# One layer of a convolution and pooling mixer: the gate rows' scaling moves to the w_out stage, the weight sums to VectorE, and two starts are reordered

## The chip, the cores and the metric

The kernel runs on one core of a Trainium2 chip. The metric is the device time of one execution in microseconds (us). The kernel before takes 1025.55 us, the median of three runs that lie between 1024.84 and 1026.43. A separate execution was recorded by the hardware profiler, and all instruction times below come from that one.

TensorE multiplies matrices into PSUM banks, VectorE and ScalarE do elementwise work (ScalarE also the activation functions), GpSimd does elementwise work and issues DMAs, and SyncE only issues DMAs. Each engine takes its instructions in the order of its own queue.

## The reference

```python
def layer(h, p, conv_hist, pool_hist, pos, ...):
    hn = rmsnorm(h, g_mix)
    proj = hn @ w_in                                    # 1024 -> 3072
    hA, bA, cA, zA, vB, zB = jnp.split(proj, 6 parts of 512)
    yA, new_conv = short_conv_mixer(hA, bA, cA, zA, conv_hist, conv_w, conv_b)
    yB, new_pool = pooling_mixer(vB, zB, pool_hist, pos, pool_w, pool_scale)
    h = h + jnp.concatenate([yA, yB], axis=-1) @ w_out  # 1024 -> 1024
    gate = jax.nn.sigmoid(rmsnorm(h, g_ple) @ w_ple_gate)
    return h + (p @ w_ple) * gate, new_conv, new_pool   # then a final rmsnorm
```

The convolution mixer is a causal width-3 convolution of `c * h`, times `b * silu(z)`. The pooling mixer takes trailing means over windows of 2, 4, 8 and 16 frames minus the frame itself, multiplies each group of 128 channels by its own 128 x 128 matrix, scales it, and multiplies by `silu(z)`. There are 2048 frames of a new stream and 32 frames of a running one, 1024 wide, all in 32-bit floats. The gate's norm weight `g_ple` belongs to the rows of `w_ple_gate`: scaling a row of the gate's weights by `g_ple` is the same as scaling the normalised frames.

## The kernel before

**Products.** Each 32-bit operand is split into a rounded high part and a low remainder: `split` (L75) casts on ScalarE (L77) and subtracts on VectorE (L78). A product is then three TensorE passes (high by high, high by low, low by high). On top of that, most products are done in the manner of Strassen and Winograd: a two-by-two block product takes seven products instead of eight, with sums and differences of the blocks formed beforehand, called S1 to S4 on one side and T1 to T4 on the other. `seven` (L197) does this for a pair of frame tiles in the w_out and gate stages: it calls `product` (L154: 12 matmuls of 512 columns), `carry` (which takes a PSUM bank out to be added later) and `out` (which adds it).

**The projection.** The frames are cut into five blocks of 416 columns, in three groups: blocks 0 and 1, blocks 2 and 3, block 4. Every group is worked through in four units, one for each 128 channels. The first unit of the first group and all four units of the last group are `plain`: full products for zb, v, c, h, za and b in this order, each with 24 matmuls of 416 columns to a block (L527). After the v product the pooling is done on VectorE (L695, L707), its result `pl` is split into `pp` (L77, L78) in a long and, in the last group, a short second piece, and `pm` (L673 to L675) multiplies `pp` by the group's matrix; in the last group `pm` stands between the h and the za products. The other units use `pair` (L802) three times, for zb with v, c with h, za with b; its carry is ScalarE's copy (L814) and its out VectorE's add (L817). Their weights come from `pair_weights` (L481): the sum `s_t` (L503) and the difference (L490) of two weight tiles run on GpSimd in the first group and on VectorE in the second. In the first group the two results are also stored to memory (`kept`, L508 and L509), and the second group loads those that were kept. Beside these units, generators work off other jobs step by step: `second_block` (L560) normalises the second block's frames and transposes them on TensorE (`turn`, L371) into the operands `B0` during the first unit; `next_columns` and `last_block` (`aside`) prepare the frames of the later groups and write them to memory with `to_memory` (L434).

**The gate's rows and other early work.** In the last group, each unit is followed in the program by `early_sums` (L943: T1 to T4 of w_out's weights, on VectorE at L164) and by two calls of `scale_gate` (L933): 128 rows of the gate's weights, 512 KB, are loaded on SyncE's queue (L939), multiplied by `g_ple` on ScalarE (L940) and stored to `g_d` from ScalarE's queue (L941). `embedding` (L100) prepares `p @ w_ple` for frame tiles: transposes (L125), cast of `pps`, 12 matmuls (L143), copy to `eout` (L145), store (L146). Four tiles (EARLY) are done before the w_out stage, 13 after it.

**The w_out stage** (from L1065). Sixteen frame tiles go in eight pairs through `seven`, then a single short tile. `prep_h` forms a pair's S operands by `frame_parts` (L167), one pair ahead. The carry adds the frames x to the PSUM bank (`c_o`, L1086). For the first pair, the top half of w_out is in SBUF already, T1 to T4 come from `early_sums`, and the bottom half (`wo_q`, L280) is loaded at its start; the 22 and 21 quarters are laid out after the first product (`rest`). After the stage come the late embedding tiles, the gate's weights read back from `g_d`, and eight pairs of the gate product with the final norm.

A scheduler orders the instructions of each engine at build time, so the order in a queue can differ from the order of the program.

Of the kernel before, what the change touches and what calls it, by code (L numbers as in the profile page):

```python
# [15 lines left out]
P = 128  # L16
D = 1024
# [12 lines left out]
EARLY = 4  # L30
# [4 lines left out]
def trunk(ctx, tc, x_p, x_s, c_conv, c_pool, p_p, p_s, g_mix, w_in, conv_w, conv_b, pool_w,  # L35
# [131 lines left out]
    def frame_parts(cmb, tmp, name, a11, a12, a21, a22):  # L167
# [19 lines left out]
        put("S1", s1)  # L187
# [9 lines left out]
    def seven(name, A, W, carry, out, between={}, late=False):  # L197
# [6 lines left out]
        X, Y, Z = (bank(f"{c}_{name}") for c in "xyz")  # L204
        product(X, A["11"], W["11"], P, True)
# [13 lines left out]
        product(Z, A["S1"], W["T1"], P, True)  # L219
        c3 = carry(Z, (1, 1))  # L220
# [67 lines left out]
    with ExitStack() as s1:  # L288
# [37 lines left out]
        gm_row = ring4(raws, "gm_row")[:1]  # L326
# [107 lines left out]
        def to_memory(mem, name, src, at, n):  # L434
            t = xin.tile([P, KH, 2, P], F32R, tag="t", name=name)
            put(t[:, :, :, :n], src)
            nc.gpsimd.dma_start(mem[:, :, :, at:at + n], t[:, :, :, :n].bitcast(F32))
# [43 lines left out]
        def pair_weights(gi, ka, kb, j, name, ring, s_ring):  # L481
# [8 lines left out]
            sub = lambda e, o, x, y: e.tensor_tensor(o, x, y, op=ALU.subtract)  # L490
# [8 lines left out]
            else:  # L499
                rb = raw_weight(kb, j, f"{name}b", ring)  # L500
                a21, a22 = rb[:, :KH], rb[:, KH:]
                eng = nc.gpsimd if gi == 0 else nc.vector
                eng.tensor_tensor(s_t, a21, a22, op=ALU.add)  # L503
                sub(eng, a21, a11, a21)
# [7 lines left out]
            def make(q):  # L512
                if q == "S2":
                    sub(nc.vector, a11, s_t, a11)
                if q == "S4":
                    sub(nc.vector, a12, a12, a11)
                t = wtile(f"w_{name}_{q}")
                put(t, src[q])
                return t
# [40 lines left out]
        def second_block():  # L560

            spans = [(c, slice(c * P, min(NB, c * P + P))) for c in range(4)]
            xs = []
            for c, cs in spans:
                x, lo, n = short0, DEC, DEC
                if c < 3:
                    x, lo, n = x_tile(f"1_{c}", [x_rows(1, c)]), 0, P
                    normal(x)
                xs.append((x, slice(lo, lo + n)))
                for half, q in enumerate(("12", "22")):  # L570
                    put(B0[q][:, :, :, cs], turn(x, half, f"pt1_{c}_{half}")[:, :, xs[c][1]])
                yield
# [50 lines left out]
        class Unit:  # L623
# [98 lines left out]
            def plain(self):  # L722
# [21 lines left out]
                if len(tbs) > 1:  # L744

                    wc = weights("c", j, f"c{tag}")
                    for b in blocks:
                        zb_block(b)
                        v_block(b)
                        if b:  # L750
                            self.mix(b - 1)
                            next(second)
                        c_block(b)
                        if b == 0:
                            for _ in range(4):
                                next(second)
# [176 lines left out]
        def scale_gate(k):  # L933

            t = ring4(raws, f"gs_{k}")
            nc.sync.dma_start(t, w_gate.rearrange("(q k c) n -> k q c n", q=4, k=KC)[k])  # L939
            nc.scalar.activation(t, t, AF.Copy, scale=vec[:, 100 + k:101 + k])  # L940
            nc.scalar.dma_start(g_d[k * P:k * P + P], t)  # L941

# [21 lines left out]
        def early_embedding():  # L964
# [3 lines left out]
            def ring(what, i):  # L968
                if what == "pps":
                    return pps_tile(i)  # L970
                if what == "out" and i == EARLY - 1:
# [13 lines left out]
        def next_columns(*cs):  # L985

            load_ahead(1, cs[0])
            for c, after in zip(cs, cs[1:] + (None,)):
                dst = lambda q, src, n: to_memory(p_d[q], f"{q}_1_{c}", src, c * P, n)
# [32 lines left out]
        for gi, tbs in enumerate(GROUPS):  # L1022
# [17 lines left out]
            for j in range(4):  # L1040
# [25 lines left out]
    with ExitStack() as s2:  # L1066
        pool = lambda name, bufs: s2.enter_context(tc.tile_pool(name=name, bufs=bufs, reuse_waits="tile"))
        w3, st, xh, qa, ss, cmb = (pool(*a) for a in (
            ("w3", 1), ("st", 4), ("xh", 3), ("qa", 2), ("ss", 3), ("cmb", 8)))
# [260 lines left out]
```

## Time and profile before

| | |
|---|---|
| median of three runs | 1025.55 us |
| the profiled execution, its own time | 1027.12 us |
| its span | 1025.3 us |
| TensorE matmuls busy | 950.1 us, 93% |
| VectorE busy | 718.8 us, 70% |
| ScalarE busy | 477.7 us, 47% |
| GpSimd busy | 152.0 us, 15% |
| mean granted TensorE clock | 0.972 |
| mean DMA rate | 185 GB/s |

The span is what the profile covers; the device time is 1.8 us more. In the rows that the prediction shows, a row of the timeline gives the start, the time that the group of instructions spans, the engine (SPq and ACTq are the DMA issues of a queue), the line, the operation, the tile written and the tiles read, the shapes, and how many instructions are in it; in brackets stands how long the engine was idle just before and what ended that. A row of the table of waits says who waited for whom, how long in all, how often, and the longest one. The granted clock is the share of full speed that TensorE had.

### The profile page before, as it was taken

What the parts mean: (1) busy time and instruction counts of PE and PEld (TensorE: products, weight loads), DVE (VectorE), ACT (ScalarE), POOL (GpSimd) and SP (SyncE); (2) the same over time, 40 slices, a digit from 0 to 9 for tenths busy, and PEclk for the clock granted to TensorE, in tenths of its full rate; (3) what the DMA queues carried; (4) which work ended last, traced back from release to release, by engine and by line L of the source; (5) the groups of instructions that cost most, each with busy time, mean ns of one, the idle gap of its engine ahead of it and who ended that gap; (6) DMA issues with size and microseconds to landing.
All of it is one profiled execution on the core that took longest, in us unless ns stands there. A gap on an engine that the chain in (4) does not pass through costs nothing. (4 is left out here: it accounts for less than half of the span.)

```text
span 1025.3 us, 13116 instructions
## 1 busy us (share of the span) xinstructions
PE 950.1 (93%) x4631; PEld 848.0 (83%) x4631; DVE 718.8 (70%) x1181; ACT 477.7 (47%) x874; POOL 152.0 (15%) x260
## 2 busy tenths in 40 slices
PE   7899998988999999997787897999999989999995
PEld 6899898978999999997787885788887768888883
DVE  6598798969576777675445464965653686888874
ACT  6454454534444544443343345433332685555553
POOL 2214433530100110000000000100000000211212
PEclk9999999999999999999799899999999999999998
DMA  9236586593954556345755738546246574665651
GB/s 258 53 125 186 158 269 192 176 283 119 421 194 133 163 163 199 119 176 162 217 157 161 209 122 325 165 158 211 89 158 197 191 284 137 215 233 184 206 196 51
DMA packets 127951, 190.03 MB, mean 185 GB/s; under 512 B 8268, under 2 KB 97612, under 8 KB 126605
## 3 DMA queue, kind: packets, MB, share of 16 engines
q1 hardware_dynamic: 115805, 137.34, 42.5%
q0 software_dynamic: 10352, 45.56, 13.0%
q10 hardware_dynamic: 1728, 6.29, 1.7%
q8 instruction: 36, 0.59, 0.2%
q14 instruction: 30, 0.25, 0.1%
HBM read 129.06 MB, written 60.10 MB: 184 GB/s over the span
## 5 line engine op out<-in xcount | busy, mean ns | idle before, releaser
L527 PE MATMUL x_ch<-B,w_ch_S 128*128 128x416 f32 x168 | 37.1, 374 | 6.5 <-ACT c_s L814 6.5
L77 ACT CAST y_S<-y_fS 128x512 fp32r<-128x512 f32 x32 | 19.6, 622 | 46.2 <-PE x_o L154 27.6
L143 PE MATMUL e<-wq,pps 128*128 128x512 f32 (+1 forms) x156 | 40.0, 408 | 0.5 <-ACT pps L77 0.5
L527 PEld LDWEIGHTS x_ch<-B,w_ch_S 128*128 128x128 f32 x168 | 33.7, 202 | 7.7 <-ACT c_s L814 7.2
L527 PE MATMUL x_zbv<-B,w_zbv_S 128*128 128x416 f32 x168 | 35.3, 360 | 3.0 <-ACT zs L814 3.0
L154 PE MATMUL x_o<-wo_b,y_S 128*128 128x512 f32 x128 | 35.9, 393 | 1.1 <-DVE c_o L1086 1.1
L364 DVE SCALAR_TENSOR_TENSOR xt<-xt,rstd_x,g_bc 128x1024 f32<-128x1024 f32 (+2 forms) x18 | 23.1, 1282 | 18.0 <-POOL rstd_x L73 16.7
L154 PE MATMUL x_g<-wg_b,g_S 128*128 128x512 f32 x128 | 35.5, 389 | 0.0
L527 PEld LDWEIGHTS x_zbv<-B,w_zbv_S 128*128 128x128 f32 x168 | 31.9, 192 | 4.1 <-ACT zs L814 3.7
L527 PE MATMUL z_zbv<-B,w_zbv_S 128*128 128x416 f32 x168 | 34.8, 357 | 0.0
L69 POOL TENSOR_SCALAR ms_f<-ssq_f 128x1 f32<-128x1 f32 x16 | 9.1, 571 | 173.1 <-ACT junk L88 173.1
L143 PEld LDWEIGHTS e<-wq,pps 128*128 128x128 f32 (+1 forms) x156 | 28.3, 189 | 7.4 <-ACT pps L77 0.8
L527 PE MATMUL z_ch<-B,w_ch_S 128*128 128x416 f32 x168 | 34.4, 354 | 0.0
L527 PE MATMUL x_zab<-B,w_zab_S 128*128 128x416 f32 x168 | 34.1, 351 | 0.0
L527 PE MATMUL z_zab<-B,w_zab_S 128*128 128x416 f32 x168 | 34.0, 351 | 0.0
L673 PE MATMUL pm<-pp,pw 128*128 128x416 f32 x20 | 7.8, 399 | 27.2 <-ACT pp L77 27.2
L527 PEld LDWEIGHTS z_zbv<-B,w_zbv_S 128*128 128x128 f32 x168 | 32.0, 192 | 0.4
L527 PEld LDWEIGHTS z_ch<-B,w_ch_S 128*128 128x128 f32 x168 | 31.7, 190 | 0.4
L527 PEld LDWEIGHTS z_zab<-B,w_zab_S 128*128 128x128 f32 x168 | 31.4, 188 | 0.3
L527 PEld LDWEIGHTS x_zab<-B,w_zab_S 128*128 128x128 f32 x168 | 31.4, 188 | 0.3
L78 DVE TENSOR_TENSOR pp<-pl,pp 128x832 fp32r<-128x832 f32 (+3 forms) x17 | 11.3, 665 | 28.2 <-ACT pp L77 28.2
L77 ACT CAST y<-y 128x512 fp32r<-128x512 f32 x24 | 14.8, 623 | 34.4 <-PE x_o L154 19.1
(533 smaller groups left out, 2737.3 us busy)
## 6 DMA issues: line engine op xcount, KB each, us to landing
y<-y_d SPq DMA_DIRECT2D x16, 512.0 KB
x<-in_x_prompt_dram SPq DMA_DIRECT2D x16, 512.0 KB
h_d<-x SPq DMA_DIRECT2D x16, 512.0 KB
h<-h_d SPq DMA_DIRECT2D x16, 512.0 KB
e<-e_d SPq DMA_DIRECT2D x16, 512.0 KB
out_dram<-h POOLq DMA_DIRECT2D x16, 512.0 KB, 3.0
xt<-in_x_prompt_dram SPq DMA_DIRECT2D x15, 512.0 KB
p_dT<-T POOLq DMA_DIRECT2D x12, 512.0 KB, 5.7
```

The source lines that it names most:

```text
L69: nc.gpsimd.tensor_scalar(ms[:n], ssq[:n], scalar1=1.0 / D, scalar2=EPS, op0=ALU.mult, op1=ALU.add)
L77: ins = nc.scalar.copy(hi, src)
L78: eng.tensor_tensor(lo, src, hi.bitcast(F32), op=ALU.subtract)
L143: nc.tensor.matmul(ps[:n], pps[:, a, k, :n], wp[k][b][:, cs], start=k + q == 0, stop=k == 1 and q == 2)
L154: nc.tensor.matmul(ps[:n], lhs[:, k, a, :n], w[b][:, k], start=start and k + q == 0, stop=k == KH - 1 and q == 2, skip_group_check=True)
L364: nc.vector.scalar_tensor_tensor(xt[:n], xt[:n], r[:n], g_bc[:n], op0=ALU.mult, op1=ALU.mult)
L527: nc.tensor.matmul(ps[:, :NB], lhs[:, k, x], b[:, k, y], start=start and k + q == 0, stop=stop and k == KH - 1 and q == 2, skip_group_chec ...
L673: nc.tensor.matmul(pm[:, :NB], pw[:, 0, j], pp, start=True, stop=False)
```

## The change

Seven parts:

1. `scale_gate` goes from the last group of the projection to the w_out stage. For each of the eight pairs, the 128 rows of one k are loaded in two halves of 512 columns, on GpSimd's queue, into the two buffers of the pool `qa`. The scaling on ScalarE and the store follow a pair later, behind the preparation of the next pair, with the scaling kept in program order.
2. `pair_weights` uses VectorE for the sum and the difference in every group (18 instructions of 128 x 512 in the first group).
3. `second_block` gets three steps of its own for loading and normalising, transposes its first round through the six product banks (`bank`) instead of the two others, and its eleven steps stand at other places: two behind zb, two behind v and three behind c of the first block, the other four as before.
4. EARLY is 3 instead of 4, so one embedding tile is done late; the early `eout` tiles use weight slots; the row of `g_mix` is loaded to another buffer.
5. The first w_out pair does its S1 by T1 product first (`t1_first`); as its x is not added in the carry (`bare`, a ScalarE copy), VectorE adds it later. The second x tile is loaded ahead of w_out's bottom half.
6. The seven 32-column pieces of the last column in `next_columns` share two staging tiles.
7. The pools of the w_out stage are opened in another order.

In the order that the scheduler builds, SyncE now issues the loads of w_out's bottom half behind the second x tile, a store of y, and the loads of the next pair's y and x, which were behind it before. On ScalarE, in the last group's second and third units, the cast of the next unit's `w_zb` stands ahead of the short second piece of `pp`.

```diff
-EARLY = 4
+EARLY = 3
...
         s1 = comb("S1", a21, a22, ALU.add)
+        if t1_first:
+            put("S1", s1)
         put("11", a11)
...
+        def lower():
+            product(Z, A["S1"], W["T1"], P, True)
+            return carry(Z, (1, 1))
+
+        if t1_first:
+            c3 = lower()
         product(X, A["11"], W["11"], P, True)
...
-        product(Z, A["S1"], W["T1"], P, True)
-        c3 = carry(Z, (1, 1))
+        if not t1_first:
+            c3 = lower()
...
-            sub = lambda e, o, x, y: e.tensor_tensor(o, x, y, op=ALU.subtract)
+            sub = lambda o, x, y: nc.vector.tensor_tensor(o, x, y, op=ALU.subtract)
...
-                eng = nc.gpsimd if gi == 0 else nc.vector
-                eng.tensor_tensor(s_t, a21, a22, op=ALU.add)
-                sub(eng, a21, a11, a21)
+                nc.vector.tensor_tensor(s_t, a21, a22, op=ALU.add)
+                sub(a21, a11, a21)
...
+            for c in range(3):
+                x = x_tile(f"1_{c}", [x_rows(1, c)])
+                normal(x)
+                xs.append((x, slice(0, P)))
+                yield
+            xs.append((short0, slice(DEC, 2 * DEC)))
             for c, cs in spans:
-                x, lo, n = short0, DEC, DEC
-                if c < 3:
-                    x, lo, n = x_tile(f"1_{c}", [x_rows(1, c)]), 0, P
-                    normal(x)
-                xs.append((x, slice(lo, lo + n)))
+                x = xs[c][0]
                 for half, q in enumerate(("12", "22")):
-                    put(B0[q][:, :, :, cs], turn(x, half, f"pt1_{c}_{half}")[:, :, xs[c][1]])
+                    put(B0[q][:, :, :, cs], turn(x, half, f"pt1_{c}_{half}", bank)[:, :, xs[c][1]])
                 yield
...
                         zb_block(b)
+                        if b == 0:
+                            for _ in range(2):
+                                next(second)
                         v_block(b)
                         if b:
                             self.mix(b - 1)
                             next(second)
+                        else:
+                            for _ in range(2):
+                                next(second)
                         c_block(b)
                         if b == 0:
-                            for _ in range(4):
+                            for _ in range(3):
                                 next(second)
...
                 if gi == 2:
                     early_sums(j)
-                    for k in range(2 * j, 2 * j + 2):
-                        scale_gate(k)
...
-        def h_ops(x, n, name):
+        def h_ops(x, n, name, bare=None):
             def carry(ps, at):
                 t = st.tile([P, NH], F32, tag="t", name=f"c_{name}_{at[0]}{at[1]}")
+                if at == bare:
+                    nc.scalar.copy(t[:n], ps[:n])
+                    return t
                 nc.vector.tensor_tensor(t[:n], ps[:n], half_of(x, at, n), op=ALU.add)
                 return t
 
             def out(ps, c, at):
                 t = half_of(x, at, n)
+                if at == bare:
+                    nc.vector.tensor_tensor(t, t, c[:n], op=ALU.add)
+                    c = None
                 nc.vector.tensor_tensor(t, ps[:n], t if c is None else c[:n], op=ALU.add)
...
+        def scale_gate(k):
+            ts = [qa.tile([P, NH], F32, tag="q", name=f"gs_{k}_{half}") for half in range(2)]
+            rows = w_gate.rearrange("(q k c) n -> k q c n", q=4, k=KC)[k]
+            for half, t in enumerate(ts):
+                nc.gpsimd.dma_start(t, rows[:, :, half * NH:half * NH + NH])
+
+            def rest():
+                for half, t in enumerate(ts):
+                    tc.keep_in_program_order(nc.scalar.activation(t, t, AF.Copy, scale=vec[:, 100 + k:101 + k]))
+                    nc.scalar.dma_start(g_d[k * P:k * P + P, half * NH:half * NH + NH], t)
+
+            return rest
+
+        second_x = load_rows(xh, "x", 1, x_p)
         bots = [cmb.tile([P, D], F32, tag="c", name=f"wo_q_{i}") for i in range(KH)]
...
         more = prep_h(0)
+        rest_gate = scale_gate(0)
         for i in range(0, NT - 1, 2):
-            x = [first_x if i + b == 0 else load_rows(xh, "x", i + b, x_p) for b in range(2)]
-            seven(f"o{i}", S.pop(i), W, *h_ops(x, P, f"o{i}"), {1: rest} if i == 0 else {}, late=True)
+            x = [load_rows(xh, "x", i + b, x_p) for b in range(2)] if i else [first_x, second_x]
+            seven(f"o{i}", S.pop(i), W, *h_ops(x, P, f"o{i}", None if i else (1, 1)), {1: rest} if i == 0 else {}, True, i == 0)
             for b in range(2):
                 done_h(i + b, x[b])
             if i + 2 < NT - 1:
                 prep_h(i + 2)()
+            rest_gate()
+            if i + 2 < NT - 1:
+                rest_gate = scale_gate(i // 2 + 1)
```

More of the change, by code (lines that the diff above doesn't have):

```diff
@@ L195, in frame_parts, with seven @@
         return A, more
-    def seven(name, A, W, carry, out, between={}, late=False):
+    def seven(name, A, W, carry, out, between={}, late=False, t1_first=False):
         step = lambda c: between[c]() if c in between else None
         X, Y, Z = (bank(f"{c}_{name}") for c in "xyz")
+        def lower():
[3 more added lines that the diff above has]
+            c3 = lower()
         product(X, A["11"], W["11"], P, True)
@@ L218, in seven @@
         step(3)
-        product(Z, A["S1"], W["T1"], P, True)
-        c3 = carry(Z, (1, 1))
+        if not t1_first:
+            c3 = lower()
         step(4)
@@ L970, in ring @@
                     return pps_tile(i)
-                if what == "out" and i == EARLY - 1:
+                if what == "out":
                     return wtile(f"eout_{i}").rearrange("p k h n -> p (k h n)").bitcast(F32)
```

34 lines of the change are left out of this document (16 added, 18 removed).

## The prediction, made before the changed kernel had run

> **What bounds the kernel now.** I read the busy time by stage first, since the page's average (TensorE 93% busy) hides where the other 7% lies. Columns of the next fence: stretch and its length, then busy time of TensorE, its weight loads, VectorE, ScalarE and GpSimd, the granted TensorE clock, DMA share, GB/s.
>
> ```profile
> 84.00:250.00 166.00, 150.09 (x771) 143.97 (x771) 138.92 (x213) 79.32 (x151) 67.99 (x74) 0.96 0.67 200
> 250.00:463.25 213.25, 213.25 (x1140) 209.79 (x1139) 155.31 (x247) 98.11 (x175) 15.71 (x25) 1.00 0.59 199
> 463.25:608.60 145.35, 118.19 (x596) 115.26 (x596) 79.22 (x182) 55.89 (x106) 5.97 (x12) 0.91 0.58 170
> 608.60:651.80 43.20, 34.30 (x139) 25.46 (x138) 24.52 (x41) 22.14 (x40) 2.27 (x5) 0.96 0.67 239
> 651.80:1014.85 363.05, 358.83 (x1611) 285.31 (x1609) 256.47 (x388) 176.86 (x315) 40.34 (x82) 1.00 0.54 186
> ```
>
> The second group of the projection (250 to 463) has no idle TensorE time, and after 651.80 only 4.22 us (363.05 - 358.83) are idle. What can be won lies in three stretches: 15.91 us idle in 84 to 250, where VectorE is busy for 84% of the time and GpSimd for 41%; 27.16 in the last group (463 to 609), where no engine but TensorE passes 55%; 8.90 at the start of the w_out stage. In all three the granted clock is below 1 too, so the idle time is not the whole loss. The table of waits names what holds the last group:
>
> ```profile
> ACT gs L940 <- DMA gs<-in_w_ple_gate_dram: 39.3, 8, 7.3
> PE pm L673 <- ACT pp L77: 27.2, 3, 11.7
> ```
>
> TensorE's pooling product `pm` waits for ScalarE's cast of `pp`, 27.2 us in three waits: that is the whole idle time of the last group. ScalarE sat idle 39.3 us ahead of the eight gate scalings.
>
> **The change, part by part.** *The gate scaling leaves the last group.* Unit 1 of it, ScalarE's rows, then SyncE's and TensorE's, then the last unit (which has no scaling ahead of `pp`):
>
> ```profile
> 524.67 1.15 ACT L940 ACTIVATE gs<-gs,vec 128x1024 f32<-128x1024 f32 x1 [7.33 <-DMA gs<-in_w_ple_gate_dram]
> 525.72 0.49 ACT L77 CAST pp<-pl 128x384 fp32r<-128x384 f32 x1
> 527.29 0.22 ACT L77 CAST pp<-pl 128x32 fp32r<-128x32 f32 x1 [1.07 <-DVE pl L707]
> 533.67 0.62 ACT L77 CAST w_zb<-raw_zb 128x512 fp32r<-128x512 f32 x1 [2.54 <-DMA raw_zb<-in_w_in_dram]
> ```
>
> ```profile
> 513.61 1.73 SPq L939 DMA_DIRECT2D gs<-in_w_ple_gate_dram  x2
> 518.63 0.38 SPq L463 DMA_DIRECT2D raw_zb<-in_w_in_dram  x1
> ```
>
> ```profile
> 527.56 0.46 PE L673 MATMUL pm<-pp,pw 128*128 128x416 f32 x1 [4.15 <-ACT pp L77]
> 528.27 6.26 PE L527 MATMUL za<-hn,w_za 128*128 128x416 f32 x24
> 534.36 4.70 PE L527 MATMUL b<-hn,w_b 128*128 128x416 f32 x24
> ```
>
> ```profile
> 596.20 0.22 ACT L77 CAST pp<-pl 128x32 fp32r<-128x32 f32 x1 [0.20 <-DVE pl L707]
> 598.54 0.35 PE L673 MATMUL pm<-pp,pw 128*128 128x416 f32 x1
> ```
>
> ScalarE's queue runs in order, so a scaling whose rows have not landed holds `pp` behind it, and `pm` holds the next 24 matmuls. Those then run at a reduced clock: 6.26 us against 4.70 for the same number. The loss is 27.2 + 3 x 1.56 = 31.9. Without the scaling the unit looks like the last one, whose cast is done at 596.42, 2.1 us before `pm` takes it at 598.54. I take 30 of the 31.9, leaving a bit for the small second cast, which was itself late by 1.07 (527.29). Upper end 31.9; the lower end is the third rival's, 7.5.
>
> *Where the scaling goes.* It is 16 ScalarE scalings of 512 columns in place of 8 of 1024; eight pairs, each with 2 x 0.57 us (half of 1.15), 2 loads and 2 stores. ScalarE is busy 176.86 of 363.05 there, so 1.15 us more in a pair is covered if the rows are there when it comes. The pair lasts seven products, and a product takes 2.72 us (649.07 to 651.79 below), 19.0 us. The load is issued about a pair ahead on GpSimd's queue, after the preceding store from the same two buffers. Two loads of 512 KB took 11.1 us from issue (513.61) to the first use (524.67), and those are twice what a pair now loads. I take 0; the ends are 0 and -20 (2.5 us uncovered in each of eight pairs), the bad case is the fourth rival. The queue also loses on SyncE: the two loads of a unit no longer stand ahead of `raw_zb`, which is issued 5 us later (518.63) and landed 15 us after that (533.67).
>
> *The first group: 18 sums of weight tiles move from GpSimd to VectorE.* TensorE's idles with the product behind each, then VectorE, then GpSimd at one such sum:
>
> ```profile
> 115.09 4.10 PE L527 MATMUL x_ch<-B,w_ch_S 128*128 128x416 f32 x12 [2.14 <-ACT c_s L814]
> 119.02 2.43 PE L527 MATMUL z_ch<-B,w_ch_S 128*128 128x416 f32 x12
> 180.29 4.09 PE L527 MATMUL x_ch<-B_T,w_ch 128*128 128x416 f32 x12 [2.36 <-DVE U L817]
> 216.62 3.50 PE L527 MATMUL x_zbv<-B,w_zbv_S 128*128 128x416 f32 x12 [2.03 <-ACT zs L814]
> 219.92 3.05 PE L527 MATMUL z_zbv<-B,w_zbv_S 128*128 128x416 f32 x12
> 234.14 3.88 PE L527 MATMUL x_ch<-B,w_ch_S 128*128 128x416 f32 x12 [4.38 <-ACT c_s L814]
> ```
>
> ```profile
> 84.05 0.68 DVE L78 TENSOR_TENSOR w_zbv_S<-raw_zbv_1b,w_zbv_S 128x512 fp32r<-128x512 f32 x1
> 84.66 1.79 DVE L490 TENSOR_TENSOR raw_zbv_1a<-raw_zbv_1a 128x512 f32<-128x512 f32 x1
> 86.37 1.28 DVE L653 COPY U<-halo_u 128x2 f32<-128x2 f32 x1
> ```
>
> ```profile
> 84.22 1.68 POOL L503 TENSOR_TENSOR s_ch<-raw_ch_1b 128x512 f32<-128x512 f32 x1 [1.52 <-DVE w_zbv_S L78]
> 85.98 1.64 POOL L490 TENSOR_TENSOR raw_ch_1b<-raw_ch_1a,raw_ch_1b 128x512 f32<-128x512 f32 x1
> ```
>
> While GpSimd adds (84.22 to 87.62), VectorE's subtraction of the same size as the row before it takes 1.79 instead of 0.68, and a copy of two columns (86.37) takes 1.28 and ends at 87.65, with GpSimd's second sum. VectorE is thus held while GpSimd computes: 1.11 us beside the first sum, about 1 us beside the second. Eighteen sums on VectorE cost it 18 x 0.68 = 12.2. Returned is some 0.9 to 1.1 for each sum that now collides, by these two rows 16 to 20 for 18; I reckon with 15, as some fall into gaps. VectorE then has about 3 us less to do, and, what matters more, no sum is waited for across two engines.
> The loss in this stretch is 15.91 idle and 6.4 of clock (1.67 + 1.66 + 1.07 + 0.62 + 1.45 over the 2.43 that a product takes at 119.02), 22.3 in all. Its releasers are ScalarE's and VectorE's carries, work behind VectorE's queue. What is late next is still VectorE, at some 136 us busy in about 152, so I take 14 of the 22.3. Upper end 22.3; lower end -12.2, all added work and nothing given back.
>
> *The second block of the first unit* is normalised three steps earlier and transposed through six banks instead of two, spread between products.
>
> ```profile
> 33.68 1.25 PE L371 MATMUL pt<-ident,xt 128*128 128x128 f32 x8 [0.96 <-DVE B L78]
> 35.74 1.26 PE L371 MATMUL pt<-ident,xt 128*128 128x128 f32 x8 [0.81 <-DVE B L78]
> 37.80 0.46 PE L371 MATMUL pt<-ident,xt 64*128 64x64 f32 x4 [0.80 <-DVE B L78]
> 39.38 6.17 PE L527 MATMUL zb<-B,w_firstzb 128*128 128x416 f32 x23
> 45.39 4.70 PE L527 MATMUL v<-B,w_firstv 128*128 128x416 f32 x24
> ```
>
> The transposes wait 2.57 us for VectorE to empty the banks, and the product behind them takes 6.17 for 23 matmuls against 4.70 for 24: 2.57 + 1.47 = 4.0. I take 3.5, between 4.0 and -1 (the banks are the products' own, and a transpose that holds one makes the next product wait one such 0.8 to 1 us).
>
> *The start of the w_out stage.* One embedding tile (12 matmuls) moves from before it to the late ones; it is executed in either place, so it costs 0. The staged loads leave ScalarE; the first pair's T1 product, whose weights are the ones summed early, goes first.
>
> ```profile
> 612.07 1.15 ACT L940 ACTIVATE gs<-gs,vec 128x1024 f32<-128x1024 f32 x1 [6.13 <-DMA gs<-in_w_ple_gate_dram]
> ```
>
> ```profile
> 614.08 0.44 PE L125 MATMUL ptp<-ident,ep 128*128 128x128 f32 x2 [2.17 <-ACT so L926]
> 618.54 5.88 PE L143 MATMUL e<-wp,pps 128*128 128x512 f32 x24 [1.22 <-ACT pps L77]
> 627.69 4.60 PE L154 MATMUL x_o<-wo_c,y 128*128 128x512 f32 x12 [3.27 <-ACT y L77]
> 649.07 2.88 PE L154 MATMUL x_o<-wo_T,y 128*128 128x512 f32 x12
> 651.79 2.88 PE L154 MATMUL x_o<-wo_c,y 128*128 128x512 f32 x12
> ```
>
> The first idle, 2.17, stands behind the scaling of 612.07 on ScalarE, the second, 1.22, behind a cast there; the third, 3.27, behind the cast of the frames, and the product after it runs 4.60 instead of 2.88. The loss is 8.90 + 1.72 = 10.6. I take 9; ends 2.2 (only the scaling's idle goes) and 10.6. The one bare copy on ScalarE, one more 512-column add on VectorE and the re-used staging buffers of the short tiles are under 1 us each beside idle engines: 0.
>
> **Sum.** 30 + 0 + 14 + 3.5 + 9 = 56.5. The profiled execution's own time is 1027.12 (span 1025.3 and 1.8 around it), so 970.6; the median of the runs is 1025.55, 1.57 lower, which gives 969.0. With every upper end (68.8) it is 956.7.
>
> [...] The product at 115.09 took 4.10 us after 2.14 idle, those at 180.29 and 216.62 lost as much after 2.36 and 2.03. [...]
>
> **The rivals.**
> *First, VectorE becomes the bound of the first group* (10%). For it: 84% busy already, and 12.2 us come on top. Against it: the stretched rows. If the stretch has another cause, that part gives -12.2 in place of 14: 995.
> *Second, the bottom half of w_out comes late* (14%). In the changed order on SyncE its loads stand behind the next pair's frames and rows, where they were ahead. Each such 512 KB costs several us; two of them, by 11.1 for two, less the 3.27 already lost, is about 8: 977.
> *Third, `pp` is still held* (12%), which is the way in which the change would not do what it says. In the changed order of ScalarE the cast of the next unit's `w_zb` stands ahead of the small second piece of `pp` in units 1 and 2. If `raw_zb` lands when it did (533.67), `pp` is 6.4 us later than at 527.29: the stall becomes 4.15 + 6.4 = 10.6 and 1.6 of clock, for two units 24.4, and that part yields 31.9 - 24.4 = 7.5: 991. Against it: `raw_zb` loses the two gate loads ahead of it.
> *Fourth, the other side: the scaling stalls ScalarE in each of the eight w_out pairs* (5%), slower. For it: in 39.3 us over eight scalings none was ever on time, and the DMA share of that stretch is 0.54, near the 0.58 of the last group. With an uncovered wait of 7.33 and 1.72 of clock in each pair, 8 x 9.05 = 72.4 is lost and 56.5 won: 1041. It decides from 5.3 us uncovered in every pair (56.5 / 8 - 1.72). Against it: 19.0 us of lead. [...]
>
> **Chances.** The forecast 57%, with its own range 959 to 981; rivals 14, 12, 10 and 5 as above; 2% for several of them at once, half of it within 0.2% (about 2 us, what a measurement of this kernel tells from no change) and half slower. The range 956 to 1000 leaves out the fourth, those 2%, and the ends. Faster is 0.92 and not 0.93, and slower 0.07, since milder stalls of the fourth's kind can add to the first or the third; the same 0.01.
>
> **What would show it.** Right: no idle of `pm` behind `pp` above 2 us in the last group, the `gs` waits of ScalarE without a TensorE idle behind them, VectorE's 128x512 rows at 0.7 in 84 to 250 and its busy time there below 140, the first w_out pair ended some 56 us earlier. Wrong: ScalarE waiting for `gs` between w_out products, VectorE above 90% with TensorE waiting on it, or `pp` behind a `w_zb` cast.

## The result and the profile after

The changed kernel takes 960.97 us (median of four runs, 960.0 to 964.14). The ratio to the kernel before is 0.9375, with a 95% interval of 0.9346 to 0.9405: 64 us less, where 56.5 were forecast. The profiled execution took 960.0 us, with a span of 958.2. A fourth run of the kernel before took 1081.71 us and is left out of the ratio as a slow one.

The first fence is the changed kernel's busy time by stage (columns as in the prediction), the second that of the kernel before, cut at the same events: the start of the second unit, of the last group, of the embedding before the w_out stage, the end of the first w_out pair, the last matmul. The later stages of the kernel before stand in the prediction, cut within 0.1 us of these events.

```profile
0.00:78.40 78.40, 72.43 (x395) 66.79 (x396) 64.15 (x117) 42.94 (x83) 15.96 (x59) 1.00 0.56 157
78.40:440.00 361.60, 356.06 (x1896) 348.16 (x1895) 284.31 (x468) 176.35 (x325) 54.52 (x81) 0.99 0.65 208
440.00:551.90 111.90, 111.90 (x597) 110.37 (x597) 79.39 (x183) 51.13 (x101) 6.00 (x12) 1.00 0.54 161
551.90:586.00 34.10, 29.59 (x124) 22.33 (x123) 25.14 (x42) 18.77 (x35) 3.87 (x7) 1.00 0.85 261
586.00:948.80 362.80, 360.05 (x1625) 286.17 (x1624) 255.75 (x388) 186.30 (x334) 50.32 (x96) 1.00 0.65 208
```

```profile
0.00:86.60 86.60, 77.99 (x395) 70.83 (x396) 63.81 (x112) 43.03 (x83) 19.40 (x61) 0.98 0.50 143
86.60:463.20 376.60, 360.69 (x1896) 351.14 (x1895) 291.58 (x456) 177.37 (x326) 81.39 (x98) 0.98 0.62 199
```

Stage by stage, the change in us: up to the second unit 86.6 to 78.4 (8.2 less), the rest of the first and second group 376.6 to 361.6 (15.0 less), last group 145.5 to 111.9 (33.6 less), embedding and first w_out pair 43.1 to 34.1 (9.0 less, but with one embedding tile fewer), the remaining pairs and the gate stage 363.0 to 362.8 (with that tile), the tail 10.5 to 9.4. The last group has no idle TensorE time left and full clock. Unit 2 of it, TensorE's rows:

```profile
481.47 4.69 PE L539 MATMUL h<-hn,w_h 128*128 128x416 f32 x24
486.00 0.35 PE L687 MATMUL pm<-pp,pw 128*128 128x416 f32 x1
486.56 4.69 PE L539 MATMUL za<-hn,w_za 128*128 128x416 f32 x24
```

`pm` follows h without a gap, and za takes 4.69 where it took 6.26. What became of the gate rows' loads in the w_out stage is told by who waits for the tile `gs`, by the time from issue to landing of its loads alone (L1139), and by ScalarE's timeline:

```profile
  ACT gs L1143: 0.5, 1
DMA to landing us min/median/max: 6.9/8.8/15.8
```

```profile
602.57 0.62 ACT L77 CAST y<-y 128x512 fp32r<-128x512 f32 x1 [2.10 <-PE z_o L154]
603.10 0.72 ACT L1143 ACTIVATE gs<-gs,vec 128x512 f32<-128x512 f32 x1
603.73 1.04 ACT L88 ACTIVATE junk<-x 128x1024 bf16<-128x1024 f32 x1
```

The loads are still slow (8.8 us for 256 KB), but ScalarE reaches the scaling long after they have landed: it waited 0.5 us in all. What is left of idle TensorE time between start and tail is mostly in these five places:

```profile
171.57 0.64 PE L539 MATMUL x_zab<-B,w_zab_S 128*128 128x416 f32 x2 [1.88 <-ACT V L834]
172.90 3.59 PE L539 MATMUL x_zab<-B,w_zab_S 128*128 128x416 f32 x10 [0.69 <-DVE w_zab_S L78]
217.82 3.97 PE L539 MATMUL z_ch<-B,w_ch_S 128*128 128x416 f32 x12 [2.62 <-ACT U L834]
562.44 3.31 PE L154 MATMUL z_o<-wo_a,y_S 128*128 128x512 f32 x12 [1.69 <-ACT y_S L77]
771.90 0.66 PE L1229 MATMUL pth<-ident,ho 128*128 128x128 f32 x4 [1.40 <-DVE pps L78]
```

### The profile page after: what moved, and what is told of

It reads as the page before. It is cut to its first block, busy times and chain, and to the rows that moved or that the text cites. A ratio compares the mean times of both kernels' runs of the same rounds, so it can differ in the third digit from the quotient of the medians.

```text
span 958.2 us, 13167 instructions
## 1 busy us (share of the span) xinstructions
PE 930.1 (97%) x4631; PEld 833.8 (87%) x4631; DVE 711.9 (74%) x1199; ACT 478.0 (50%) x883; POOL 133.4 (14%) x258
## 4 chain that ended last, share of the span: by engine, by line
PE 69%; DMA 7%; DVE 3%; ACT 2%; issue 1%; POOL 0%; POOLq 0%; SPq 0%; ACTq 0%; DVEq 0%
PE x_g L154 9%; PE x_o L154 8%; PE x_zab L539 5%; PE z_g L154 5%; PE z_o L154 4%; PE x_ch L539 4%; PE x_zbv L539 4%; PE z_zab L539 2%; PE z_ch L539 2%; PE y_g L154 2%; DMA wg_r<-g_d 2%; PE z_zbv L539 2%; PE y_o L154 2%; PE b L539 2%; PE v L539 2%; PE zb L539 2%
## 5 line engine op out<-in xcount | busy, mean ns | idle before, releaser
L539 PE MATMUL x_zbv<-B,w_zbv_S 128*128 128x416 f32 x168 | 34.1, 351 | 0.0
L539 PE MATMUL x_ch<-B,w_ch_S 128*128 128x416 f32 x168 | 34.0, 351 | 0.0
L1101 DVE TENSOR_TENSOR c_o<-x_o,x 128x512 f32<-128x512 f32 x16 | 11.1, 692 | 28.0 <-PE x_o L154 28.0
L539 PEld LDWEIGHTS x_ch<-B,w_ch_S 128*128 128x128 f32 x168 | 31.4, 188 | 0.3
L1268 DVE SCALAR_TENSOR_TENSOR h<-h,rstd_f,g_bc 128x1024 f32<-128x1024 f32 x16 | 20.6, 1284 | 12.4 <-POOL rstd_f L73 12.3
L154 PEld LDWEIGHTS x_o<-wo_b,y_S 128*128 128x128 f32 x128 | 24.0, 188 | 6.0 <-ACT y L77 1.3
```

Source lines behind the costliest of these rows:

```text
L154: nc.tensor.matmul(ps[:n], lhs[:, k, a, :n], w[b][:, k], start=start and k + q == 0, stop=k == KH - 1 and q == 2, skip_group_check=True)
L539: nc.tensor.matmul(ps[:, :NB], lhs[:, k, x], b[:, k, y], start=start and k + q == 0, stop=stop and k == KH - 1 and q == 2, skip_group_chec ...
L1268: nc.vector.scalar_tensor_tensor(h[:n], h[:n], rf[:n], g_bc[:n], op0=ALU.mult, op1=ALU.mult)
```

## The experiments

Times of experiments are compared by their ratio to the kernel before, which ran beside each; "us slower than the changed kernel" is the difference of the two ratios times 1025.6. The interval of one ratio is about 0.003 to either side, 3 us.

### What the gate rows cost, and why

**Back into the last group, on ScalarE.**

```diff
+        def scale_gate(k):
+            t = ring4(raws, f"gs_{k}")
+            nc.sync.dma_start(t, w_gate.rearrange("(q k c) n -> k q c n", q=4, k=KC)[k])
+            nc.scalar.activation(t, t, AF.Copy, scale=vec[:, 100 + k:101 + k])
+            nc.scalar.dma_start(g_d[k * P:k * P + P], t)
...
                     early_sums(j)
+                    for k in range(2 * j, 2 * j + 2):
+                        scale_gate(k)
...
-        rest_gate = scale_gate(0)
...
-            rest_gate()
-            if i + 2 < NT - 1:
-                rest_gate = scale_gate(i // 2 + 1)
```

> The changed kernel with the gate rows' scaling put back into the last group of the projection (512 KB loads on SyncE, scaling on ScalarE, store from ScalarE's queue); all else stays changed. Theory (ScalarE's queue holds pp behind the landing of the gate rows): the three waits of pm for pp return, about 27 us idle and 5 to 6 of clock, with some more at the start of the w_out stage: 961 + 33 to 38 = 994 to 999. Rival (the other parts removed the cause as well, so the place of the scaling matters little): below 975.

Measured: 1011.06 us, ratio 0.9854 (0.9815 to 0.9892), 49 us slower than the changed kernel and above the 994 to 999 expected. The wait came back as expected:

```profile
PE pm L687 <- ACT pp L77: 30.1, 3, 12.4
```

The last group (start of its first zb to the first embedding product) takes 148.5 us against 112.1. The rest, for which I had allowed only a little, is the start of the w_out stage: from the first embedding product to the end of the first pair 47.3 us against 34.0.

**The same place, but scaled on GpSimd.** As above, with

```diff
-            nc.scalar.activation(t, t, AF.Copy, scale=vec[:, 100 + k:101 + k])
-            nc.scalar.dma_start(g_d[k * P:k * P + P], t)
+            nc.gpsimd.tensor_scalar(t, t, scalar1=vec[:, 100 + k:101 + k], scalar2=None, op0=ALU.mult)
+            nc.gpsimd.dma_start(g_d[k * P:k * P + P], t)
```

> As the run before it, the gate rows loaded and scaled in the last group, but the scaling and its store are on GpSimd's queue instead of ScalarE's. Theory (it is the order in ScalarE's queue that cost the time): pm does not wait for pp, 961 to 966. Rival (the slow gate loads themselves delay the loads of the units' weights, which share the DMA engines and SyncE's queue with them): TensorE waits for zb, v and c instead, 975 to 995.

Measured: 1001.63 us, ratio 0.9759 (0.9725 to 0.9793), 39 us slower than the changed kernel. My theory does not hold: with ScalarE's queue free of the scaling, most of the loss stays (the last group takes 143.6 us). The rival is right about the cause, late weights, but the time lies above its 975 to 995, and TensorE waits for the `st` copies and not for zb, v and c. First TensorE's two largest waits, then SyncE and ScalarE around the first of them:

```profile
PE pst L944 <- DVE st L936: 15.6, 3, 6.9
PE pm L687 <- ACT pp L77: 6.9, 2, 5.3
```

```profile
452.56 1.74 SPq L955 DMA_DIRECT2D gs<-in_w_ple_gate_dram  x2
457.71 0.40 SPq L476 DMA_DIRECT2D raw_zb<-in_w_in_dram  x1
```

```profile
469.82 1.14 ACT L77 CAST w_zb<-raw_zb 128x512 fp32r<-128x512 f32 x2 [11.81 <-DMA raw_zb<-in_w_in_dram]
```

`raw_zb`, issued behind the two gate loads, lands 12 us after its issue (3.8 in the changed kernel), and ScalarE now idles 11.8 us for it. VectorE waits for that cast (its `st` copies stand behind it), TensorE for VectorE. So the gate loads did two things: they held ScalarE's queue, and they held the weights issued behind them. That GpSimd's scaling slows VectorE instead is not what the trace shows: VectorE is busy 78.7 us in the last group, and 79.4 in the changed kernel.

**The kernel before, with the same loads in another shape.**

```diff
-            nc.sync.dma_start(t, w_gate.rearrange("(q k c) n -> k q c n", q=4, k=KC)[k])
+            rows, n = w_gate.rearrange("(q k c) n -> k q c n", q=4, k=KC)[k], P // 4
+            for q in range(4):
+                nc.sync.dma_start(t[q * n:q * n + n], rows[q])
```

> The kernel before, unchanged but for the shape of the gate rows' load: four loads of 32 consecutive rows each on SyncE instead of one load of four times 32 rows; scaling on ScalarE in the last group, as before. Theory (the one-piece load is slow by its pattern, 0.2 to 0.3 of the DMA engines busy while two of them run, and keeps the unit's weights waiting as well): the rows land in 4 to 5 us, the three waits of pm fall from 27 us to below 6, and the time by 25 to 35: 990 to 1000. Rival (the scaling is late whatever the shape, because 512 KB more are moved in a busy stretch): 1012 to 1026.

Measured: 994.33 us, ratio 0.9693 (0.9662 to 0.9725): 31.5 us won on the kernel before by an edit of the load alone, half of what the whole change wins. The first fence is the kernel before: the mean busy share of the 16 DMA engines from 513 to 530 us in 40 slices of 0.43 us, in tenths, and SyncE's row of `raw_v`; the two gate loads are issued at 513.61, `raw_zb` at 518.63, `raw_v` at 519.33. The second is the reshaped load: who waits for `gs`, and the loads' time to landing; the third its wait of `pm`, and unit 1 on ScalarE.

```profile
DMA  0000131122331223599999842222222257999999
519.33 6.70 SPq L463 DMA_DIRECT2D raw_v<-in_w_in_dram  x1
```

```profile
  DMA gs<-in_w_ple_gate_dram: 0.8, 1
DMA to landing us min/median/max: 2.3/2.8/5.3
```

```profile
PE pm L673 <- ACT pp L77: 3.2, 2, 3.0
...
505.19 0.52 ACT L77 CAST pp<-pl 128x384 fp32r<-128x384 f32 x1 [1.47 <-DVE pl L707]
508.21 0.21 ACT L77 CAST pp<-pl 128x32 fp32r<-128x32 f32 x1
510.37 1.15 ACT L942 ACTIVATE gs<-gs,vec 128x1024 f32<-128x1024 f32 x1
```

While only the gate loads run, the mean busy share is 0.1 to 0.3; when `raw_zb` and `raw_v` come, it is 0.8 to 0.9 for nearly 3 us, then 0.2 to 0.4 for another 4 us, and it rises to 0.9 again from about 526.6. SyncE's row goes with that: issuing `raw_v` takes 6.70 us, until 526.03, where `raw_zb` took 0.38 and `raw_v` takes 0.38 in the changed kernel. So the weights are held up already while they are issued. The shares are means over the 16: which engines were busy, and why the others were not, the trace does not show. With 32 consecutive rows to a load, a piece (a quarter of one) lands in 2.8 us, and ScalarE waits 0.8 us in all instead of 39.3.

The edit changed more than the shape, though. With it, the scheduler put both casts of `pp` ahead of the unit's first scaling in each of units 0 to 2, as the rows of unit 1 show (in the kernel before, 524.67 stands ahead of 525.72). How the 31.5 us divide between the faster load and this order, no run tells. That the order is not needed for most of the loss, the run before this one shows: there ScalarE has no scaling in its queue, and the last group still takes 143.6 us.

**Reshaped and in place, in the changed kernel.** The changed kernel with the first diff of this section, and its load as in the last one.

> The changed kernel with the gate scaling back in the last group, on ScalarE, but loaded in four pieces of 32 consecutive rows. Theory (the load's shape was the trouble, the place is not): within 6 us of the changed kernel, 958 to 967, against 1011 with the one-piece load at the same place. Rival (the place matters too, through ScalarE's queue and w_out's start): 970 or more.

Measured: 980.23 us, ratio 0.9558 (0.9527 to 0.9589), 19 us slower than the changed kernel: the rival. The last group takes 118.7 us (148.5 with the one-piece load, 112.1 in the changed kernel), so the edit mends most of it there, with the casts of `pp` ahead of the scaling again; the start of the w_out stage takes 43.8, against 34.0. TensorE and ScalarE there:

```profile
576.60 5.49 PE L154 MATMUL z_o<-wo_a,y_S 128*128 128x512 f32 x12 [6.41 <-ACT y_S L77]
```

```profile
570.02 1.15 ACT L958 ACTIVATE gs<-gs,vec 128x1024 f32<-128x1024 f32 x1 [0.60 <-DMA gs<-in_w_ple_gate_dram]
572.91 0.33 ACTq L959 DMA_DIRECT2D g_d<-gs  x1
575.57 0.33 ACTq L146 DMA_DIRECT2D e_d<-eout  x1
575.93 0.62 ACT L77 CAST y_S<-y_fS 128x512 fp32r<-128x512 f32 x1 [4.29 <-DMA e_d<-eout]
```

The gate's and the embedding's last stores are issued from ScalarE's queue at 572.91 and 575.57, and the cast that the first pair needs comes behind them, where ScalarE idled 4.29 us until a store of the embedding was done. On the kernel before the same is seen in part: with the reshaped load in place, this stretch takes 40.5 us, with the scaling moved away 36.2, a difference of 4.4 where it is 9.9 here. So the last unit's scaling costs there even with the faster load; through which of the queue's instructions, and why more in the changed kernel, was not taken apart.

**The move alone, on the kernel before.** Only the first part of the change (the diff of `scale_gate`, `rest_gate` and the two lines removed from the last group).

> The kernel before with the first part of the change alone: the gate rows' scaling in the w_out stage, a pair behind its load, loads on GpSimd's queue in the old pattern. Theory: it wins what the reshaped load won in place (32 us), and perhaps 1 to 4 more, as the waits of pm go altogether: 988 to 995. Rival (with w_out's start as it was, the loads on GpSimd's queue delay the first pair): 995 to 1005.

Measured: 984.96 us, ratio 0.9602 (0.9576 to 0.9627): 40.8 us of the 64. By stage: the last group 145.6 to 112.1 us, embedding and first pair 42.9 to 36.2. I had expected 30 to 37 us, and had the start of the w_out stage too low; the gate move makes both.

### The weight sums

**Back on GpSimd**, in the changed kernel:

```diff
-                nc.vector.tensor_tensor(s_t, a21, a22, op=ALU.add)
-                sub(a21, a11, a21)
+                eng = nc.gpsimd if gi == 0 else nc.vector
+                eng.tensor_tensor(s_t, a21, a22, op=ALU.add)
+                eng.tensor_tensor(a21, a11, a21, op=ALU.subtract)
```

> The changed kernel with the 18 weight sums of the first group back on GpSimd. Theory (the sums on GpSimd hold VectorE): VectorE's 128x512 rows beside them are at 1.2 to 1.8 us again, TensorE has about 10 us more idle time and some clock loss in 78 to 440, 961 + 13 to 17 = 974 to 978. Rival (the stalls of that group came from the staging of frames, which the shared tiles of the short pieces mended): below 965.

Measured: 969.76 us, ratio 0.9455 (0.9426 to 0.9484), 8.2 us slower than the changed kernel. First and second group take 371.7 us against 361.6, so 10 us there; the expected 13 to 17 was too much.

**Sums on VectorE, and 18 additions on GpSimd that nobody reads.**

```diff
+        scratch = wk.tile([P, KH, P], mybir.dt.bfloat16, tag="scratch", bufs=1, name="scratch")
...
+                    for read in (s_t, s3):
+                        nc.gpsimd.tensor_tensor(scratch, read, g_bc[:, :NH].rearrange("p (k n) -> p k n", k=KH), op=ALU.add)
                     nc.gpsimd.dma_start(k1, s_t)
                     nc.gpsimd.dma_start(k3, s3)
```

> The changed kernel, sums on VectorE, with 18 additions of 128 x 512 added on GpSimd behind them at the places where the sums stood, whose results nobody reads. Theory one (while GpSimd adds, VectorE is held, whoever needs the sum): VectorE's rows beside them stretch to 1.2 to 1.8 us, its busy time in the first group rises by 15 to 20 us, and the time by 8 to 25: 969 to 986. Theory two (the cost was the wait of VectorE and ScalarE for a sum made on another, slower engine): no stretch and 960 to 963.

Measured: 971.49 us, ratio 0.9467 (0.9439 to 0.9495), 9.4 us slower than the changed kernel, by work that no one waits for. Two of the additions on GpSimd, and what VectorE did at the time:

```profile
118.69 1.28 POOL L522 TENSOR_TENSOR scratch<-raw_zbv_2b,g_bc 128x512 bf16<-128x512 f32 x1 [1.23 <-issue]
...
145.22 1.61 POOL L522 TENSOR_TENSOR scratch<-raw_ch_2b,g_bc 128x512 bf16<-128x512 f32 x1 [0.18 <-issue]
```

```profile
118.97 1.02 DVE L676 COPY halo_u<-U 128x2 f32<-128x2 f32 x1
...
145.60 1.78 DVE L504 TENSOR_TENSOR raw_ch_2a<-s_ch,raw_ch_2a 128x512 f32<-128x512 f32 x1
147.41 0.69 DVE L504 TENSOR_TENSOR raw_ch_2a<-raw_ch_2a 128x512 f32<-128x512 f32 x1
```

A subtraction of the same size takes 1.78 beside the addition and 0.69 just after it, and the copy of two columns 1.02. In the rest of the first and second group VectorE is busy 295.2 us, 10.9 more than in the changed kernel (15 to 20 were expected). Theory one holds: it is GpSimd's adding that holds VectorE, not the wait for the sum. The useless additions cost no less than the real ones, which leaves little for the wait. (They also stand ahead of the `kept` stores in GpSimd's queue; how much of the 9.4 us that is was not taken apart.)

**Sums on VectorE alone, on the kernel before.**

```diff
-                eng = nc.gpsimd if gi == 0 else nc.vector
+                eng = nc.vector
```

> The kernel before with the 18 weight sums of the first group on VectorE and nothing else changed. Theory (GpSimd's additions hold VectorE): 8 to 11 us less, 1015 to 1018, VectorE's busy time down although it does more. Rival (VectorE, 12 us more work in order, becomes the bound without the other parts): 1024 or more.

Measured: 1017.32 us, ratio 0.9917 (0.9889 to 0.9945), 8.5 us less. First and second group:

```profile
82.60:448.60 366.00, 356.49 (x1896) 347.61 (x1895) 284.91 (x470) 176.62 (x325) 56.68 (x83) 0.99 0.65 205
```

VectorE has 14 instructions more in its count (470 against 456) and is busy 284.91 us against 291.58: it does more in less time, as expected. The stage went from 376.6 to 366.0.

### The second block, the staging tiles and the first pair

**The second block as before** (the diff of `second_block` and its places undone).

```diff
-                    put(B0[q][:, :, :, cs], turn(x, half, f"pt1_{c}_{half}", bank)[:, :, xs[c][1]])
+                    put(B0[q][:, :, :, cs], turn(x, half, f"pt1_{c}_{half}")[:, :, xs[c][1]])
...
                         if b == 0:
-                            for _ in range(3):
+                            for _ in range(4):
```

> The changed kernel with the second block as before (normalised and transposed in one step, two banks, four steps behind c). Theory (the banks and the pile of steps behind c cost the clock as well as the idle time, 6.8 us from the c product to the second unit): 961 + 5 to 7 = 966 to 968. Rival (most of those 6.8 us come with the earlier start and the other parts): 961 to 964.

Measured: 966.15 us, ratio 0.9417 (0.9387 to 0.9447), 4.3 us slower than the changed kernel. The intervals overlap at their edges; in the profile the second unit starts at 84.67 instead of 78.42, and 59.7 us after the first c product instead of 52.7 (59.5 in the kernel before).

**Only the banks as before**, the steps spread as changed (the first of these two edits alone).

> The changed kernel with the second block's first transposes through two banks again, but normalised ahead and spread over the products as changed. Theory one (the banks are what matters): 2 to 5 us slower, 963 to 966, waits of the transposes for VectorE return. Theory two (the spreading between products is what matters): 960 to 962.5.

Measured: 964.28 us, ratio 0.9400 (0.9376 to 0.9424), 2.6 us slower than the changed kernel, inside the uncertainty of the two ratios. The transposes wait for VectorE again, as in the kernel before, but the product behind them takes 4.62 us for its 23 matmuls, against 6.17 in the kernel before (39.38) and 4.51 in the changed one (34.75):

```profile
32.96 1.25 PE L381 MATMUL pt<-ident,xt 128*128 128x128 f32 x8 [0.81 <-DVE B L78]
35.02 0.46 PE L381 MATMUL pt<-ident,xt 64*128 64x64 f32 x4 [0.81 <-DVE B L78]
36.61 4.62 PE L539 MATMUL zb<-B,w_firstzb 128*128 128x416 f32 x23
```

The second unit starts at 82.04, 56.1 us after the first c product. Counted from that product, whose own start differs from run to run, the banks account for 3.4 us and the places of the steps for 3.7 by the profiles; the times alone do not separate the two.

**A staging tile for each short piece**, as before.

```diff
-                dst = lambda q, src, n: to_memory(p_d[q], f"{q}_1_{c}", src, c * P, n, next(places) if n == DEC else None)
+                dst = lambda q, src, n: to_memory(p_d[q], f"{q}_1_{c}", src, c * P, n)
```

> The changed kernel with a staging tile of its own for each of the seven 32-column pieces. The part of the first and second group's gain that the sums do not account for is 361.6 against 371.7 us with the sums on GpSimd and 376.6 before. Theory (the staging buffers held the frames' preparation, 5 us): 964 to 967. Rival (those 5 us are the scheduler's other order): 960 to 963.

Measured: 964.74 us, ratio 0.9403 (0.9375 to 0.9431), 2.9 us slower than the changed kernel, which the intervals do not separate. First and second group take 365.6 us against 361.6, and ScalarE has a wait for a store out of such a buffer that the kernel before has too (3.9 us) and the changed kernel lacks:

```profile
ACT T L77 <- DMA p_d<-21_1_3_1043: 3.6, 1, 3.6
```

So the theory is likely, at 3 to 4 us, and not proved by the times.

**The first pair in the old order of products.**

```diff
-            S[i], more = frame_parts(cmb, ss, f"y{i}", lo[:, :, :P], hi[:, :, :P], lo[:, :, P:], hi[:, :, P:], i == 0)
+            S[i], more = frame_parts(cmb, ss, f"y{i}", lo[:, :, :P], hi[:, :, :P], lo[:, :, P:], hi[:, :, P:])
...
-            seven(f"o{i}", S.pop(i), W, *h_ops(x, P, f"o{i}", None if i else (1, 1)), {1: rest} if i == 0 else {}, True, i == 0)
+            seven(f"o{i}", S.pop(i), W, *h_ops(x, P, f"o{i}", None), {1: rest} if i == 0 else {}, True)
```

> The changed kernel with the first w_out pair in the old order of products (S1 by T1 in the fifth place, carry with x), the other loads as changed. Theory one (the order T1 first covers the layout of w_out's bottom half, which lands late): the first pair waits 3 to 8 us more, 964 to 970. Theory two (the start was held by the gate scaling alone): 960 to 963.

Measured: 961.44 us, ratio 0.9366 (0.9340 to 0.9392): no difference. Embedding and first pair take 33.8 us against 34.0. T1 first does nothing here; theory two.

## Why the prediction was right, and where it was not

969.0 was forecast and 961.0 measured; the direction, the range (956 to 1000) and the likeliest case's own range (959 to 981) held. By its terms, with the profile's stages:

- *Last group, 30 of at most 31.9:* 33.6. The size was right and a little low; the upper end left out that the `pm` matmuls themselves ran slowly behind the idle (0.72, 0.55 and 0.55 us at 493.20, where 0.35 each is usual). The mechanism was half of it. That `pp` stood behind the scaling in ScalarE's queue is what the trace showed and what stalled first; but taking the scaling off that queue left 39 us of loss in place, 31.5 of it in the last group, since the weights issued behind the one-piece load were late too. Reshaping the load won 31.5 us with the scaling left in the group and on ScalarE, though in another order. The prediction took the slowness of these loads (11.1 us for two) only as a danger for the w_out stage; it did not see in it a cause of the stall.
- *Where the scaling goes, 0:* right. ScalarE waited 0.5 us for the rows in eight pairs, so the fourth rival did not come, though the loads take 8.8 us each (and a scaling 0.71 where 0.57 was reckoned). GpSimd's queue, which waits for the stores (30.7 us in 13 waits), has nothing behind them that is urgent.
- *First group, 14 of 22.3:* the stages give 15.0, but it is 10 for the sums (10.1 and 10.6 us in the two runs) and about 4, likely for the staging tiles, which the prediction put at 0. Its price for the sums was too high and another part's too low, and that the sum came out is luck. What it said mattered more, that no sum is waited for across two engines, is not what won: additions that nobody waits for cost as much. The first rival fell: VectorE's busy time went down.
- *Second block, 3.5, at most 4.0:* the term that was mis-sized. The profile gives 8.2 up to the second unit, 6.8 of it from the first c product on (59.5 to 52.7); the run with the old block needs 59.7 there, and its time is 4.3 us more. The step counted the transposes' idle time (2.57) and the lost clock in the zb product only. Of the 6.8, 3.1 are idle TensorE time and 3.7 slower work, at a granted clock of 0.97 against 1.00: the eight-transpose groups ran slowly as well, 1.25 us each where the changed kernel does 24 in 2.55. The run with two banks and spread steps shows that the pile of steps behind c costs about as much as the banks. The other 1.4 of the 8.2 lie ahead of that product and belong to neither: in the profiles of kernels that are the same up to that point (the kernel before, the sums alone, the gate move alone), the first c product starts anywhere between 24.9 and 27.1.
- *Start of the w_out stage, 9:* 9.0 in the profile, of which about 3 is only the moved embedding tile (late ones follow each other after 2.97 us), so 6 where 9 was forecast. The gate move alone gave 6.7 (42.9 to 36.2). T1 first, which the prediction named among the reasons for this term, gave nothing. The tile that went to the late embedding cost nothing visible: the remaining stages take 362.8 against 363.0 with it. So some 3 us were won there that the prediction did not have; TensorE idles 2.8 us there instead of 4.2, and the rest was not taken apart.
- *Second and third rival:* neither came. `wo_q`'s loads stand behind the next pair's in SyncE's order, and cost an idle of 0.84 us and one of 0.23; `pm` has no idle at all, although the cast of `w_zb` stands ahead of the small piece of `pp`, because `raw_zb` no longer waits behind the gate loads.

From one profiled execution to the other the time fell by 67.1 us (1027.1 to 960.0), 10.6 more than the sum of the terms: 4.7 up to the second unit, 3.6 in the last group, 1.0 in the first and second, 1.1 in the tail and 0.2 elsewhere. In the first group, and in the w_out stage with what follows it, the total came near its forecast only because one part's miss made up for another's. The medians are 8 us from the forecast, as the profiled execution lay 1.6 us above the median before and 1.0 below it after.

## What to carry to other kernels

When an engine waits for a load, look first at how long the load takes against another of the same size and at the DMA engines' share while it runs: here two loads of four times 32 rows in one piece kept the engines' mean busy share at 0.1 to 0.3, and weights issued behind such loads landed after 12 us instead of 3.8; cutting each into four of 32 rows, with the order that the scheduler then chose, won 31.5 us, half of all that a seven-part change did. Such an edit can change the order of the queues too, so compare the order before calling the load alone the cause. A wait named in the trace can have a second one behind it on another queue, so a test that moves only the named one (here, scaling on another engine) is worth its run. Additions on GpSimd beside a busy VectorE are not free even when their result is not needed: 18 of them cost 9 us of a TensorE-bound kernel.

## What the runs showed of the hardware that was not expected

**GpSimd's additions hold VectorE, for a copy too.** A VectorE copy of 128 x 2, 0.15 us by itself (halo_u in the changed kernel at 169.93), took 1.02 us (118.97, above) and 1.28 us (86.37 in the kernel before) beside one. By what means the one engine holds the other, no run here shows. GpSimd's scaling of one tile held nothing: here it is beside VectorE in the run that scales the gate rows on GpSimd.

```profile
468.37 2.84 POOL L956 TENSOR_SCALAR gs<-gs,vec 128x1024 f32<-128x1024 f32 x1 [2.85 <-DMA gs<-in_w_ple_gate_dram]
470.47 0.69 DVE L78 TENSOR_TENSOR w_zb<-raw_zb,w_zb 128x512 fp32r<-128x512 f32 x1 [11.85 <-ACT w_zb L77]
```

VectorE's subtraction with two inputs takes its usual 0.69 inside the 2.84 of the scaling, and another at 587.59 takes 0.68 inside one of 3.48 (GpSimd's spans are rough in the profile). It did not wait for the scaling's end; why the two kinds of GpSimd work differ stays open.

**The same idle costs clock or not.** The prediction took each idle of 2 us and more to cost about 1.7 us of clock, from three of three in the kernel before. Here is the same product with the same 2.62 us of idle ahead, in the run with one staging tile for each short piece:

```profile
223.12 2.53 PE L539 MATMUL z_ch<-B,w_ch_S 128*128 128x416 f32 x12 [2.62 <-ACT U L834]
```

It takes 2.53 us at a granted clock of 1.00, and 3.97 at 0.58 in the changed kernel (217.82, above), where 2.43 is usual. So such an idle cost 0.1 us in one run and 1.5 in the other, and the prediction's reading was too firm. What else decides it, no run here shows.
